# Splitting the weight blocks of a hybrid encoder kernel: one instruction per part of a whole block, in place of one per part of each half

## The chip, the cores and the metric

The kernel runs on one core of one Trainium2 chip. The metric is the device time of one execution in microseconds. The kernel before took 910.26 us, the median of three runs (910.05 to 911.16). The engines of the core are named as in the profile: PE is the matrix engine (PEld its loads of the stationary operand), DVE the vector engine, ACT the scalar engine, POOL the general engine, and SP the queue that issues most of the transfers.

## What is computed

One layer of an encoder on 512 tokens of width 1024, all in float32. A combined projection feeds three mixers (a bidirectional mLSTM, a two-dimensional neighbourhood attention, a cross-attention into 256 memory tokens). Their outputs are gated, summed and projected, and a gated feed-forward block of inner width 2816 follows. Cut to what matters:

```python
h = rms_norm(x, mix_norm_g)
proj = h @ w_in                       # 1024 x 7184
...                                   # the three mixers
merged = g_ml * (y_ml @ w_br_ml) + g_na * (y_na @ w_br_na) + g_xa * (y_xa @ w_br_xa)
x = x + merged @ w_out
a, u = split(rms_norm(x, ffn_norm_g) @ w_ffn_up)      # 1024 x 5632
x = x + (gelu(dwconv3(a, w_conv, b_conv)) * u) @ w_ffn_down   # 2816 x 1024
return rms_norm(x, final_norm_g)
```

## The kernel before

**Three matmuls for one.** Every dense product is done in a float32 kind that the matrix engine reads rounded. So each operand is split into a high part (the value, rounded by a copy into that kind) and a low part (what the rounding lost), and `mm3` (line 201) issues three matmuls for each k tile of 128 rows: high weights by high input (L202), high weights by low input (L203), low weights by high input (L204). The input's parts are made once and stay in buffers called units. The weights' parts are made block by block, just ahead of their use.

**Blocks.** `block_list` (line 53) cuts all weights into 159 blocks in the order of use. Nearly all are 128 partitions by 1024 columns: for a projection these are the 8 k tiles of one output tile, side by side. The 2816 rows of the down projection are 22 k tiles, done in two passes of 11 (`HF`); one output tile in one pass takes two blocks, of 8 and of 3 k tiles (1024 and 384 columns, line 82). Three blocks called `dnl` hold the weights of the last two output tiles of the second pass; their parts go into units that are kept to the end (`lastw`, line 160).

**A block's way.** `emit_raw` (line 141) loads a block into one of 3 raw buffers by a transfer that SP issues. `emit_split` (line 167) makes the parts, half a block at a time: for a half of 512 columns one ACT copy writes the high part (L184), and one DVE subtraction writes the low part (L185). Each half has a buffer of its own; there are 4 for the high and 4 for the low parts, of 544 columns each (`HWD`). `weights(key)` (line 190) is called just before a block's matmuls. It emits loads up to three blocks ahead and splits up to one block ahead.

**Order.** The program is written in one order, but a scheduler reorders each engine's instructions by when it expects them to be ready, earlier written ones first, and gives a buffer to the next user when it expects it to be free. An engine then runs its list strictly in that order. A split of a half can start when some buffer has been released by the last matmul that read it: L203 for a high part, L204 for a low part.

**The stages**, by the trace: the q and k projections and the values (to about 98 us), the projections of the mixers with the mLSTM's steps between them (to 310), the gates with the neighbourhood attention between them (to 420), the last gates and the output projection (to 531), and the feed-forward block. There `ua` and `uu` are the two halves of the up projection, one block each per tile `f`, and `dn` is the down projection: 11 tiles of `ua` and `uu` to 655, 8 tiles of `dn` to 716, 11 tiles of `ua` and `uu` to 838, and 5 of `dn` to 876. From there the last three output tiles are done in halves of 256 columns and rows, with the final norm between (`last_tiles`, line 980).

Two places differ from the regular course. At tile `f` = 0 of the up projection (lines 1088 to 1104) both blocks are in use at once: 7 k tiles of `ua`, 7 of `uu`, then the last of `ua`, eight small matmuls for the norm (L283), and the last of `uu`. And in the stage of the values, `mem_part` (line 393) loads and splits the memory tokens in four steps (L396, L398, L208, L209) on the same engines as the weights.

Of the kernel before, what the change touches and what calls it, by code (L numbers as in the profile page):

```python
# [11 lines left out]
F32 = mybir.dt.float32  # L12
F32R = mybir.dt.float32r
AF = mybir.ActivationFunctionType
ALU = mybir.AluOpType
AX = mybir.AxisListType

P = 128
# [7 lines left out]
HF = FT // 2  # L26
# [5 lines left out]
EPS = 1e-6  # L32
NEG = -1e30
BW = 1088
HWD = 544
UNIT = 2064
ROWS, GW = 8, 64
CW = (0, 8, 24, 32)
# [14 lines left out]
def block_list():  # L53

    L = []
    for i in range(4):
        L.append((("mlq", i), 1024))
    for f in range(4):
        L.append((("mlk", f), 1024))
    for c in range(4):  # L60
        n = 272 if c == 0 else 256
        for h in range(2):
            L.append((("tm", c, h), 4 * n))
    for n in ("xaq", "o", "memk", "memv", "naq", "nak"):
        for f in range(4):
            L.append(((n, f), 1024))
    for br in range(3):
        for fp in range(4):
            L.append((("g", br, 2 * fp), 1024))
            L.append((("g", br, 2 * fp + 1), 1024))  # L70
            L.append((("br", br, fp), 1024))
    for f in range(8):
        L.append((("out", f), 1024))
    for hh in range(2):
        for f in range(HF * hh, HF * (hh + 1)):
            L.append((("ua", f), 1024))
            L.append((("uu", f), 1024))
        for f in range(8 if hh == 0 else LF):
            if hh == 1 and f >= LF - 3:
                i = f - LF + 3  # L80
                L.append((("dnl", i), 256 * (4 if i < 2 else 3)))
            for i, n in ((0, 8), (1, 3)):
                L.append((("dn", hh, f, i), n * 128))
    return L


BLOCKS = block_list()
BINDEX = {}
_off = 0
# [4 lines left out]
BCOLS = {n: (lambda k: P) for n in ("mlk", "o", "xaq", "memk", "naq", "nak", "g", "out", "ua", "uu", "dn")}  # L94
# [7 lines left out]
def hybrid_block(ctx, tc, xT, memT, wflat, vecs, gbias, nabias, outa, outb):  # L102
    nc = tc.nc
    V, A, G, PE, SY = nc.vector, nc.scalar, nc.gpsimd, nc.tensor, nc.sync

    cp = ctx.enter_context(tc.tile_pool(name="cp", bufs=1))
    wp = ctx.enter_context(tc.tile_pool(name="wp", bufs=3))
# [9 lines left out]
    def nm(s):  # L117
        uid[0] += 1
        return f"{s}_{uid[0]}"

    def unit(dt=F32):
        return up.tile([P, UNIT], dt, tag="unit", name=nm("u"))
# [14 lines left out]
    raws, split = {}, {}  # L137
# [11 lines left out]
            return [(r[:, a:b], src[:, a:b]) for a, b in zip(cuts, cuts[1:])]  # L149
        SY.dma_start(r[:, :n], src)  # L150

    def halves(i):
        n, c = BLOCKS[i][1], BCOLS[BLOCKS[i][0][0]](BLOCKS[i][0])
        k = n // c
        k0 = k if n <= HWD else (k + 1) // 2
        return c, [(0, k0)] + ([(k0, k)] if k0 < k else [])

    lw = []

    def lastw(k, m):  # L160

        if not lw:
            lw.extend(unit(F32R) for _ in range(4))
        q = slice(k % 8 * 256, k % 8 * 256 + m)
        return lw[k // 8][:, q], lw[2 + k // 8][:, q]

    def emit_split(i):
        key, n = BLOCKS[i]
        r = raws.pop(i)
        c, hs = halves(i)  # L170
        split[i] = []
        for a, b in hs:
            m = (b - a) * c
            if key[0] == "dnl":
                h, l = lastw(4 * key[1] + a, m)
            else:
                h = wp.tile([P, HWD], F32R, tag="hi", name=nm("wh"), bufs=4)
                l = wp.tile([P, HWD], F32R, tag="lo", name=nm("wl"), bufs=4)
            for u, v in ((0, P), (P, m)) if i == 0 and a == 0 else ((0, m),):
                src = r[:, a * c + u:a * c + v]  # L180
                if i == 0 and a == u == 0:
                    V.tensor_copy(h[:, u:v], src)
                else:
                    A.activation(h[:, u:v], src, AF.Copy)  # L184
                V.tensor_tensor(l[:, u:v], src, h[:, u:v].bitcast(F32), op=ALU.subtract)  # L185
            for k in range(a, b):
                q = slice((k - a) * c, (k - a + 1) * c)
                split[i].append((h[:, q], l[:, q]))

    def weights(key):  # L190

# [67 lines left out]
    for d in range(2):  # L259
        sgn = 1 if d == 0 else -1  # L260
        m = cp.tile([P, P], F32, name=f"msk{d}")
# [81 lines left out]
    for k in range(KT):  # L343
# [5 lines left out]
        wh, wl = ws[k % 2]  # L349
# [64 lines left out]
    for c in range(4):  # L414
        if c == 3:
            mem_part()
        n = 272 if c == 0 else 256
# [467 lines left out]
    for f in range(4):  # L885
        ps = proj(("naq", f), XH, XL)
        V.tensor_tensor(nq[:, f * S:(f + 1) * S].rearrange("p (b r c) -> p b r c", r=ROWS, b=4), rv(ps), rv(rb),
                        op=ALU.mult)
# [15 lines left out]
    for br in range(3):  # L904
# [8 lines left out]
        for fp in range(4):  # L913
            tg = []
            for i in range(2):
                f = 2 * fp + i
# [11 lines left out]
            for i in range(2):  # L928
                f = 2 * fp + i
# [152 lines left out]
    for hh in range(2):  # L1082
# [3 lines left out]
        for j in range(HF):  # L1086
            f = HF * hh + j
            if f == 0:
# [7 lines left out]
                k = KT - 1  # L1096
# [8 lines left out]
            c = conv(pa, rb2, "ffw", "ffb", f, FT)  # L1105
# [33 lines left out]
def _layout(inp):  # L1139
    w_in = inp["w_in"][0]  # L1140
    o_ml = 0
    c_q, c_k, c_v, c_o = 0, 512, 1024, 1536
    c_g = 2048
    c_nq, c_nk, c_nv = 2064, 2064 + 512, 2064 + 1024
    c_xq = 2064 + 1536
    c_m = c_xq + 512
    wi = _tiles(w_in)
    mkv = _tiles(inp["w_mem_kv"][0])
    br = [_tiles(inp[n][0]) for n in ("w_br_ml", "w_br_xa", "w_br_na")]
    wo = _tiles(inp["w_out"][0])  # L1150
    wu = _tiles(inp["w_ffn_up"][0])
    wd = _tiles(inp["w_ffn_down"][0])
    parts = []
    for key, n in BLOCKS:
        kind = key[0]
        if kind == "mlq":
            b = wi[:, 2 * key[1]:2 * key[1] + 2, c_q:c_q + 512]
        elif kind in ("mlk", "o", "xaq", "naq", "nak"):
            c = {"mlk": c_k, "o": c_o, "xaq": c_xq, "naq": c_nq, "nak": c_nk}[kind] + key[1] * P
            b = wi[:, :, c:c + P]  # L1160
        elif kind == "tm":
            _, c, h = key
            ks = slice(4 * h, 4 * h + 4)
            if c == 0:
                b = np.concatenate([wi[:, ks, c_g:c_g + 16], wi[:, ks, c_v:c_v + 256]], axis=2)
            elif c == 1:
                b = wi[:, ks, c_v + 256:c_v + 512]
            else:
                b = wi[:, ks, c_nv + (c - 2) * 256:c_nv + (c - 1) * 256]
        elif kind == "memk":  # L1170
            b = mkv[:, :, key[1] * P:(key[1] + 1) * P]
        elif kind == "memv":
            b = mkv[:, 2 * key[1]:2 * key[1] + 2, 512:1024]
        elif kind == "g":
            gi = (0, 2, 1)[key[1]]
            c = c_m + gi * 1024 + key[2] * P
            b = wi[:, :, c:c + P]
        elif kind == "br":
            b = br[key[1]][:, :, key[2] * 256:(key[2] + 1) * 256]
        elif kind == "out":  # L1180
            b = wo[:, :, key[1] * P:(key[1] + 1) * P]
        elif kind == "ua":
            b = wu[:, :, key[1] * P:(key[1] + 1) * P]
        elif kind == "uu":
            b = wu[:, :, DFF + key[1] * P:DFF + (key[1] + 1) * P]
        elif kind == "dnl":
            k = HF + 4 * key[1]
            b = wd[:, k:k + n // 256, LF * P:]
        else:
            _, hh, f, i = key  # L1190
            b = wd[:, HF * hh + 8 * i:HF * hh + 8 * i + n // P, f * P:(f + 1) * P]
        parts.append(np.ascontiguousarray(b).reshape(-1))
    wflat = np.concatenate(parts)

    vt = lambda a: a.reshape(-1, P).T
    vecs = np.concatenate([vt(inp["mix_norm_g"][0]), vt(inp["ffn_norm_g"][0]), vt(inp["mem_norm_g"][0]),
                           vt(inp["final_norm_g"]),
                           vt(inp["w_ml_conv"][0].reshape(-1)), vt(inp["b_ml_conv"][0]), vt(inp["b_merge_gate"][0]),
                           vt(inp["w_ffn_conv"][0].reshape(-1)), vt(inp["b_ffn_conv"][0]), vt(inp["ml_norm_g"][0])], axis=1)
    bi, bf = inp["b_ml_igate"][0], inp["b_ml_fgate"][0]  # L1200
    gbias = np.concatenate([bi[0], bf[0], bi[1], bf[1], inp["final_norm_g"][LF * P:]])

    rpb = inp["na_rpb"][0]
    q = np.arange(P)
    qr, qc = q // 16, q % 16
    kk = np.arange(M)
    kr, kc = kk // 32, kk % 32
    nab = np.empty((8, P, 4, M), rpb.dtype)
    for b in range(4):
        c = 16 * b + qc  # L1210
        cols = CW[b] + kc
        start = np.clip(c - 8, 0, GW - 16)
        ok = (cols[None, :] >= start[:, None]) & (cols[None, :] < start[:, None] + 16)
        dr = kr[None, :] - qr[:, None] + 7
        dc = np.clip(cols[None, :] - c[:, None] + 15, 0, 30)
        nab[:, :, b, :] = np.where(ok[None], rpb[:, dr, dc], rpb.dtype.type(NEG))

    xT = _tiles(np.ascontiguousarray(inp["x"][0].T))
    memT = _tiles(np.ascontiguousarray(inp["mem"][0].T))
    return {"xT": xT, "memT": memT, "wflat": wflat, "vecs": vecs, "gbias": gbias, "nabias": nab.reshape(8, P, 2, 2 * M).transpose(0, 2, 1, 3)}  # L1220
# [17 lines left out]
```

## Time and profile before

| | |
|---|---|
| runs | 910.05, 910.26, 911.16 us |
| the profiled execution's own time | 909.93 us |
| its span in the profile | 908.1 us |
| granted PE clock, mean over the span | 0.998 |
| PE busy | 900.4 us, 4502 matmuls |
| PEld busy | 755.2 us |
| DVE busy | 579.5 us, 1059 instructions |
| ACT busy | 436.8 us, 884 instructions |
| POOL busy | 107.5 us |
| read from memory | 92.57 MB, 105 GB/s with what is written |

The 1.8 us between span and time lie around the first and last recorded instruction. Matmuls overlap, so their durations (0.39 us for 512 columns) are longer than the distance between the starts of two, and it is the distance that fills the span. In rows of the timeline the columns are start in us, duration in us, engine, line, operation, output and inputs, shape, count, and in brackets the engine's idle time before it with what ended that.

### The profile page before, as it was taken

The numbers are of one execution on the slowest core, as the hardware profiler recorded it, in microseconds if no ns is written. First come the engines' busy times: TensorE is split into PE (matmuls) and PEld (weight loads), VectorE is DVE, ScalarE is ACT, GpSimd is POOL, SyncE is SP. The second block draws the span as 40 slices with busy tenths as digits, with TensorE's granted clock in tenths as the row PEclk, the third lists the DMA queues.
The fourth block names the chain that finished last, engine by engine and source line by source line (L and its number), as shares of the span: only waits on it lengthen the run. The fifth ranks groups of instructions, "written<-read, shape, count | busy, mean of one in ns | idle before, by whom it ended". The sixth has DMA issues, their size and how long they took to land.

```text
span 908.1 us, 12239 instructions
## 1 busy us (share of the span) xinstructions
PE 900.4 (99%) x4502; PEld 755.2 (83%) x4502; DVE 579.5 (64%) x1059; ACT 436.8 (48%) x884; POOL 107.5 (12%) x136
## 2 busy tenths in 40 slices
PE   9999999999999999999999999999999999999997
PEld 7899888888888888888888888888888888888887
DVE  6794656746566758885555548777733477777433
ACT  7474546755545647654334435444422244444442
POOL 4200311102040300000000221111100011111010
PEclk9999999999999999999999999999999999999999
DMA  7223543422232333232223432222233322322312
GB/s 264 96 71 119 182 119 116 156 89 82 91 119 71 114 105 127 95 117 70 93 93 117 139 116 93 93 93 92 88 96 96 116 93 93 93 93 87 119 49 93
DMA packets 33339, 96.52 MB, mean 106 GB/s; under 512 B 4344, under 2 KB 7672, under 8 KB 33280
## 3 DMA queue, kind: packets, MB, share of 16 engines
q1 hardware_dynamic: 31584, 92.32, 31.5%
q0 software_dynamic: 1408, 3.16, 1.2%
q8 instruction: 35, 0.57, 0.3%
q10 hardware_dynamic: 288, 0.27, 0.1%
q14 instruction: 24, 0.20, 0.1%
HBM read 92.57 MB, written 3.16 MB: 105 GB/s over the span
## 4 chain that ended last, share of the span: by engine, by line
PE 96%; DVE 1%; issue 1%; ACT 1%; DMA 1%; SPq 0%; POOLq 0%; POOL 0%; DVEq 0%
PE mm L202 28%; PE mm L203 28%; PE mm L204 28%; PE at L202 2%; PE at L203 2%; PE at L204 2%; PE at L580 2%; PE at L718 1%; PE at L705 1%; DMA s<-xT 1%; PE at L795 0%; PE at L688 0%; PE at L687 0%; PE at L283 0%; PE at L604 0%
## 5 line engine op out<-in xcount | busy, mean ns | idle before, releaser
L202 PE MATMUL mm<-u,wh 128*128 128x512 f32 (+1 forms) x1077 | 420.6, 391 | 0.5 <-ACT u L208 0.3
L203 PE MATMUL mm<-u,wh 128*128 128x512 f32 (+1 forms) x1077 | 417.4, 388 | 0.3 <-DVE u L209 0.3
L204 PE MATMUL mm<-u,wl 128*128 128x512 f32 (+1 forms) x1077 | 417.2, 387 | 0.0
L184 ACT ACTIVATE wh<-wr 128x512 fp32r<-128x512 f32 (+1 forms) x298 | 185.6, 624 | 285.6 <-PE mm L203 241.5
L185 DVE TENSOR_TENSOR wl<-wr,wh 128x512 fp32r<-128x512 f32 (+3 forms) x299 | 228.7, 766 | 121.4 <-ACT wh L184 114.9
L204 PEld LDWEIGHTS mm<-u,wl 128*128 128x128 f32 x1077 | 202.2, 188 | 45.2 <-DVE wl L185 0.4
L202 PEld LDWEIGHTS mm<-u,wh 128*128 128x128 f32 x1077 | 202.3, 188 | 44.2 <-ACT u L208 0.6
L203 PEld LDWEIGHTS mm<-u,wh 128*128 128x128 f32 x1077 | 202.4, 188 | 43.9 <-DVE u L209 1.3
L1111 POOL TENSOR_TENSOR s<-s,rb 128x512 f32<-128x512 f32 x22 | 29.1, 1323 | 266.4 <-DVE s L1110 258.3
L208 ACT ACTIVATE u<-s 128x512 fp32r<-128x512 f32 x34 | 21.4, 630 | 53.1 <-DVE s L1114 50.6
L964 POOL TENSOR_TENSOR acc<-acc,s 128x512 f32<-128x512 f32 x7 | 9.1, 1298 | 223.1 <-ACT s L963 223.1
L209 DVE SCALAR_TENSOR_TENSOR u<-s,u 128x512 fp32r<-128x512 f32 x34 | 23.5, 692 | 14.9 <-ACT u L208 14.6
L919 DVE TENSOR_TENSOR s<-mm,rb_x 128x512 f32<-128x512 f32 x24 | 16.6, 690 | 23.6 <-PE mm L204 23.5
L568 ACT ACTIVATE E<-R,bi 128x128 f32<-128x128 f32 x80 | 27.8, 393 | 4.2 <-POOL R L549 4.0
L369 ACT ACTIVATE s<-pad,vec 128x512 f32<-128x512 f32 x30 | 24.4, 812 | 8.3 <-DVE pad L367 8.3
L370 DVE SCALAR_TENSOR_TENSOR s<-pad,vec,s 128x512 f32<-128x512 f32 x30 | 22.5, 751 | 6.1 <-ACT s L369 6.0
L202 PE MATMUL mm<-wh,u 128*128 128x256 f32 (+1 forms) x80 | 24.5, 306 | 0.0
L203 PE MATMUL mm<-wl,u 128*128 128x256 f32 (+1 forms) x80 | 24.3, 304 | 0.0
L204 PE MATMUL mm<-wh,u 128*128 128x256 f32 (+1 forms) x80 | 24.3, 304 | 0.0
L1110 DVE SCALAR_TENSOR_TENSOR s<-s,s 128x512 f32<-128x512 f32 x22 | 15.2, 692 | 13.4 <-ACT s L1109 13.3
L371 DVE SCALAR_TENSOR_TENSOR s<-pad,vec,s 128x512 f32<-128x512 f32 x30 | 22.5, 750 | 0.7
L367 DVE TENSOR_TENSOR pad<-mm,rb 128x512 f32<-128x512 f32 x22 | 15.1, 692 | 11.6 <-PE mm L204 11.6
(261 smaller groups left out, 1003.2 us busy)
## 6 DMA issues: line engine op xcount, KB each, us to landing
wr<-wflat SPq DMA_DIRECT2D x140, 512.0 KB, 3.4
s<-xT SPq DMA_DIRECT2D x16, 256.0 KB, 4.3
nab<-nabias SPq DMA_DIRECT2D x16, 256.0 KB, 2.7
wr<-wflat SPq DMA_DIRECT2D x15, 192.0 KB, 2.4
R<-rd SPq DMA_DIRECT2D x8, 256.0 KB, 3.5
u<-nav_d POOLq DMA_DIRECT2D x32, 64.0 KB, 2.9
wr<-wflat SPq DMA_DIRECT2D x2, 544.0 KB, 3.3
s<-memT SPq DMA_DIRECT2D x4, 256.0 KB, 3.6
```

The costliest lines, as they stand in the source:

```text
L184: A.activation(h[:, u:v], src, AF.Copy)
L185: V.tensor_tensor(l[:, u:v], src, h[:, u:v].bitcast(F32), op=ALU.subtract)
L202: PE.matmul(ps, lh, rh, start=start, stop=False)
L203: PE.matmul(ps, lh, rl, start=False, stop=False)
L204: PE.matmul(ps, ll, rh, start=False, stop=stop)
L208: A.activation(h, src, AF.Copy, scale=scale)
L209: V.scalar_tensor_tensor(l, src, scale, h.bitcast(F32), op0=ALU.mult, op1=ALU.subtract)
L369: A.activation(t1, pad[:, 0:512], AF.Identity, scale=vcol(w, i), bias=vcol(b, i))
L370: V.scalar_tensor_tensor(t1, pad[:, 1:513], vcol(w, n + i), t1, op0=ALU.mult, op1=ALU.add)
L371: V.scalar_tensor_tensor(t1, pad[:, 2:514], vcol(w, 2 * n + i), t1, op0=ALU.mult, op1=ALU.add)
L568: A.activation(E[:, i, :], src, AF.Exp, bias=bi[:, d, abs(J - s), s, h:h + 1])
L1111: G.tensor_tensor(c, c, rb2, op=ALU.mult)
```

## The change

A whole block is split by one ACT copy and one DVE subtraction, into one of 2 high and 2 low buffers of 1088 columns each. Only the first two blocks are still cut, at the borders at which their transfers are cut. The blocks of the down projection hold 6 and 5 k tiles (768 and 640 columns) in place of 8 and 3. The loads, their buffers, the matmuls and everything else in the program stay as they were; the columns of the `dnl` blocks go to the same places.

```diff
-HWD = 544
+KA = 6
...
-            for i, n in ((0, 8), (1, 3)):
+            for i, n in ((0, KA), (1, HF - KA)):
                 L.append((("dn", hh, f, i), n * 128))
...
-    def halves(i):
-        n, c = BLOCKS[i][1], BCOLS[BLOCKS[i][0][0]](BLOCKS[i][0])
-        k = n // c
-        k0 = k if n <= HWD else (k + 1) // 2
-        return c, [(0, k0)] + ([(k0, k)] if k0 < k else [])
...
     def emit_split(i):
         key, n = BLOCKS[i]
         r = raws.pop(i)
-        c, hs = halves(i)
-        split[i] = []
-        for a, b in hs:
-            m = (b - a) * c
-            if key[0] == "dnl":
-                h, l = lastw(4 * key[1] + a, m)
+        c = BCOLS[key[0]](key)
+        if key[0] == "dnl":
+            h, l = lastw(4 * key[1], n)
+        else:
+            h = wp.tile([P, BW], F32R, tag="hi", name=nm("wh"), bufs=2)
+            l = wp.tile([P, BW], F32R, tag="lo", name=nm("wl"), bufs=2)
+
+        cuts = ((0, P, n // 2, n), (0, n // 2, n))[i] if i < 2 else (0, n)
+        for u, v in zip(cuts, cuts[1:]):
+            if i == u == 0:
+                V.tensor_copy(h[:, u:v], r[:, u:v])
             else:
-                h = wp.tile([P, HWD], F32R, tag="hi", name=nm("wh"), bufs=4)
-                l = wp.tile([P, HWD], F32R, tag="lo", name=nm("wl"), bufs=4)
-            for u, v in ((0, P), (P, m)) if i == 0 and a == 0 else ((0, m),):
-                src = r[:, a * c + u:a * c + v]
-                if i == 0 and a == u == 0:
-                    V.tensor_copy(h[:, u:v], src)
-                else:
-                    A.activation(h[:, u:v], src, AF.Copy)
-                V.tensor_tensor(l[:, u:v], src, h[:, u:v].bitcast(F32), op=ALU.subtract)
-            for k in range(a, b):
-                q = slice((k - a) * c, (k - a + 1) * c)
-                split[i].append((h[:, q], l[:, q]))
+                A.activation(h[:, u:v], r[:, u:v], AF.Copy)
+            V.tensor_tensor(l[:, u:v], r[:, u:v], h[:, u:v].bitcast(F32), op=ALU.subtract)
+        split[i] = [(h[:, k:k + c], l[:, k:k + c]) for k in range(0, n, c)]
...
-            b = wd[:, HF * hh + 8 * i:HF * hh + 8 * i + n // P, f * P:(f + 1) * P]
+            b = wd[:, HF * hh + KA * i:HF * hh + KA * i + n // P, f * P:(f + 1) * P]
```

## The prediction

> **What bounds the kernel now.** I read the page first, then the waits, then the groups by shape, then the timeline at the places where the change could bite.
>
> ```profile
> span 908.1 us, 12239 instructions
> PE 900.4 (99%) x4502; PEld 755.2 (83%) x4502; DVE 579.5 (64%) x1059; ACT 436.8 (48%) x884; POOL 107.5 (12%) x136
> PE 96%; DVE 1%; issue 1%; ACT 1%; DMA 1%; SPq 0%; POOLq 0%; POOL 0%; DVEq 0%
> L204 PEld LDWEIGHTS mm<-u,wl 128*128 128x128 f32 x1077 | 202.2, 188 | 45.2 <-DVE wl L185 0.4
> ACT wh L184 <- PE mm L203: 241.5, 176, 3.8
> DVE wl L185 <- ACT wh L184: 114.9, 105, 4.2
> ```
>
> The matrix engine is busy from end to end, and 96% of the chain that ended last is matmuls. The weight parts are not what it waits for: loads of low parts lost 0.4 us to the split in the whole run. It is the other way round: ACT stood 241.5 us waiting until matmuls released a high buffer. So a cheaper split buys nothing by itself. The time can move only through two things: stalls of PE that a later split would bring, and the distance between matmuls that follow each other without a stall.
>
> **What a split costs, narrow and wide.**
>
> ```profile
> L184 ACT ACTIVATE wh<-wr 128x512 fp32r<-128x512 f32 x279 | 175.1, 629 | 262.8 <-PE mm L203 223.2 <-DMA wr<-wflat 10.2 <-issue 9.5
> L184 ACT ACTIVATE u<-wr 128x256 fp32r<-128x256 f32 x1 | 0.4, 401 | 0.0
> L185 DVE TENSOR_TENSOR u<-wr,u 128x512 fp32r<-128x512 f32 x5 | 3.4, 690 | 5.6 <-ACT u L184 5.6
> L185 DVE TENSOR_TENSOR u<-wr,u 128x256 fp32r<-128x256 f32 x1 | 0.4, 424 | 0.0
> L1121 DVE TENSOR_TENSOR u<-mm,u 128x512 f32<-128x512 f32 x13 | 9.0, 692 | 14.8 <-PE mm L204 14.8
> wr<-wflat SPq DMA_DIRECT2D x140, 512.0 KB, 3.4
> ```
>
> No row has 1024 columns. From 256 to 512 columns ACT adds 0.228 us and DVE 0.266 us, so the wide ones take 0.629 + 2 x 0.228 = 1.08 us and 0.690 + 2 x 0.266 = 1.22 us. The bounds are no fixed part at all, twice the narrow one (1.26 and 1.38 us), and, below, the narrow one itself. For 768 and 640 columns the same line gives 0.86 and 0.74 us on ACT, 0.96 and 0.82 on DVE. Some 0.17 us of ACT and 0.16 us of DVE are saved for each block; both lie beside matmuls and are worth nothing.
>
> **How late a block becomes.** A row of the steady course, block `uu` of a tile and the block after it:
>
> ```profile
> 588.10 0.63 ACT L184 ACTIVATE wh<-wr 128x512 fp32r<-128x512 f32 x1 [0.18 <-PE mm L203]
> 588.72 1.28 POOL L1111 TENSOR_TENSOR s<-s,rb 128x512 f32<-128x512 f32 x1 [8.69 <-DVE s L1110]
> 588.76 1.78 DVE L185 TENSOR_TENSOR wl<-wr,wh 128x512 fp32r<-128x512 f32 x1
> 593.57 0.40 PE L202 MATMUL mm<-u,wh 128*128 128x512 f32 x1
> 599.18 0.39 PE L202 MATMUL mm<-u,wh 128*128 128x512 f32 x1
> 604.67 0.40 PE L202 MATMUL mm<-u,wh 128*128 128x512 f32 x1
> 610.28 0.39 PE L202 MATMUL mm<-u,wh 128*128 128x512 f32 x1
> ```
>
> 593.57 starts the `uu` block, 599.18 the `ua` block, 604.67 `uu` again. The second half of the 593.57 block got its buffer at 588.10, where the block two before ended. Its first half had got its own half a block earlier. In the new kernel all of it begins at 588.10: high part ready at 589.2, low part at 590.4, or 591.5 with the 1.09 us (1.78 less 0.69) that the subtraction loses beside POOL. It is needed at 593.57, its low part at 594.0. Before, the second half was ready at 588.73 (high) and 590.54 (low) for a use half a block after 593.57, at 596.4: a slack of 7.6 and 5.8 us. It falls to 4.4 and 2.5, and no stall follows. What is queued behind the longer wait are the evacuations and the activation chain on ACT and DVE; they get 0.5 us more delay, and the matmuls that need their results (the down projection) come many blocks later. The raw buffer comes free about 1 us later, so SP's next load starts that much later; it takes 3.4 us and has two blocks of time.
>
> [...]
>
> In the down projection a block has 6 k tiles or 5. Twenty-four matmuls take 5.5 us, so 6 k tiles take 4.2 and 5 take 3.5. The 6-tile block's buffer is released 3.5 us before its use: 3.5 - 0.86 - 0.96 leaves 1.7 us. The 5-tile block has 4.2 us, less 0.74, 0.82 and one evacuation of 0.69 on DVE: 1.9 us. No stall, with 8 and 3 or with 6 and 5.
>
> **Two places with less room.** First, tile 0 of the up projection, where two blocks are held together.
>
> ```profile
> 541.59 0.63 ACT L184 ACTIVATE wh<-wr 128x512 fp32r<-128x512 f32 x1 [2.11 <-PE mm L203]
> 542.69 0.69 DVE L185 TENSOR_TENSOR wl<-wr,wh 128x512 fp32r<-128x512 f32 x1
> 543.23 0.39 PE L202 MATMUL mm<-u,wh 128*128 128x512 f32 x1
> 543.68 0.39 PE L204 MATMUL mm<-u,wl 128*128 128x512 f32 x1
> ```
>
> At 541.59 the last k tile of `ua` gave its buffer back. The block needed at 543.23 had been split before; with two buffers it can only start then. High part 541.59 + 1.08 = 542.67, low part to 543.95 with a small instruction between, wanted at 543.68. A stall of **0.35 us** (0 with the narrow duration, 0.7 with the doubled ones).
>
> Second, the step from the values to the mixers:
>
> ```profile
> 97.52 0.63 ACT L184 ACTIVATE wh<-wr 128x512 fp32r<-128x512 f32 x1
> 101.57 0.63 ACT L398 ACTIVATE s<-s 128x512 f32<-128x512 f32 x1 [2.88 <-DMA s<-memT]
> 102.91 1.66 ACT L184 ACTIVATE wh<-wr 128x512 fp32r<-128x512 f32 x3
> 103.59 0.39 PE L202 MATMUL mm<-u,wh 128*128 128x512 f32 x1
> 104.05 0.39 PE L204 MATMUL mm<-u,wl 128*128 128x512 f32 x1
> 104.11 1.28 DVE L185 TENSOR_TENSOR wl<-wr,wh 128x512 fp32r<-128x512 f32 x2
> ```
>
> The first half of the block used at 103.59 was copied at 97.52; its second half stood in ACT's list behind the last step of the memory tokens, whose load came late, to 102.91. The whole block now goes to one of these two places. Ahead: no stall. Behind: high part 102.91 + 1.08 = 103.99, low part 104.11 + 1.22 = 105.33, wanted at 104.05: 1.3 us, or 1.9 if the later raw release pushes the memory load behind it by 0.6. I take **0**: ACT is idle when the buffer comes free (97.52 to 101.57 holds one short evacuation besides), and a scheduler that takes what is ready would fill that. The other value is a rival.
>
> **The distance between matmuls.** The rows from 599.18 to 604.67 and on to 610.28 hold the same work: 24 matmuls of 512 columns, the same inputs, no stall. `ua` takes 5.49 us and `uu` 5.61, tile after tile. What differs is where the weights lie. Tile 0 shows it: the release at 541.59 is of the second buffer of `ua`, taken out of turn. Counting the buffers as they come free, `ua` since then sits in buffers 0 and 2 and `uu` in 1 and 3. Buffers are 544 columns apart, so in units of 32 columns they start at 0, 17, 34 and 51: `ua` in the even places, `uu` in the odd. In the new kernel the halves of the two buffers start at 0, 16, 34 and 50, all even. If the place is the cause, all 22 `uu` blocks take `ua`'s time: 21 x 0.12 = **-2.5 us** (tile 0 left out). The other end is that all go at `uu`'s pace: +2.6 us.
>
> More rows show the down projection, a projection of the mixers, and the first of the last tiles:
>
> ```profile
> 860.80 0.39 PE L202 MATMUL mm<-u,wh 128*128 128x512 f32 x1
> 868.43 0.39 PE L202 MATMUL mm<-u,wh 128*128 128x512 f32 x1
> 123.32 0.39 PE L202 MATMUL mm<-u,wh 128*128 128x512 f32 x1
> 126.11 0.39 PE L202 MATMUL mm<-u,wh 128*128 128x512 f32 x1
> 128.87 0.40 PE L202 MATMUL at<-u,u 128*128 128x512 f32 x1
> 876.03 0.28 PE L202 MATMUL mm<-u,wh 128*128 128x256 f32 x1
> 878.39 0.28 PE L204 MATMUL mm<-u,wl 128*128 128x256 f32 x1
> ```
>
> Eleven k tiles of `dn` take 7.63 us; at `ua`'s pace they would take 5.49 x 11 / 8 = 7.55. Over 13 tiles that is at most -1.0 us; I take **-0.3**, as the buffers rotate and only half the blocks lie in odd places. In the mixers' stage the first half of the block (even) takes 2.79 us and the second (odd) 2.76, the other way round than in the feed-forward block, so the place of the input counts too. Should the second halves slow down to 2.79, 44 such blocks lose 44 x 0.03 = 1.3 us; should they stay, nothing. I take **+0.6**.
>
> **The sum**, on the profiled execution's own 909.93 us: +0.35 - 2.5 - 0.3 + 0.6 = -1.85, which gives 908.1 us. The median of the runs is 0.33 us above that execution, so **908.4 us** against 910.26. The start (the first two blocks keep their cuts) and the tail are unchanged: the last 5-tile block gets its buffer at 876.03 and has both parts after 0.74 + 0.82 and an evacuation of 0.69, at 878.3; its low part is first wanted at the seventh k tile, 878.39.
>
> **The rivals.**
>
> *The place of the weights does nothing* (the 0.12 us comes from something else that stays, such as the output bank or the place of the inputs, and `uu` keeps 5.61). For it: the mixers' rows point the other way. Against it: `ua` and `uu` have the same inputs. Then only the stall is left: 910.26 + 0.35 = 910.6 us. [...] Rows of 5.49 / 24 = 229 and 5.61 / 24 = 234 ns do not agree with a single distance.
>
> *The stall at the memory tokens comes, and the spacing does not*: 910.26 + 0.35 + 1.3 to 1.9 = 911.9 to 912.5, **912.2 us**, slower. For it: the second half was put behind that step before. It decides as soon as ACT's list has the copy behind L398. With the spacing gained as well it would be 910.0.
>
> *All blocks fall into the slow class*: +2.6 in the up projection, +1.3 in the mixers' stage, +0.35: 914.5 us. For it: the even place is the slow one in the mixers' rows. Against it: the even place is the fast one in the 22 tiles.
>
> **The chances.** A measurement of this kernel tells no less than 0.2% from no change, 1.8 us. Forecast 0.45; it lies on that bound, so I count 0.33 of it as faster and 0.12 as within. Spacing unmoved: 0.27, within. Stall with or without the gain: 0.16, of it 0.11 slower, 0.03 within, 0.02 faster (the mixers' stage improving too). Slow class: 0.12, slower. Waits not foreseen, from lists put in another order, take 0.04 from "within" to slower. Together: faster 0.35, within 0.38, slower 0.27. The range goes from 906.2 (-2.5, -1.0 and -0.6 in the mixers' stage, without the stall) to 913.5, short of the slow class. The forecast's own range is 906.5 to 909.8.
>
> **What would show it.** `uu` at 5.49 us like `ua` shows the spacing right; both at 5.61, or unchanged, shows it wrong. The first copy after tile 0's first blocks should be 1.08 us long, and the wait of PE for L185 at that place 0.35 us. The copy ahead of L398 shows the second place right, behind it wrong. Splits of 1.08 and 1.22 us show the durations. A PE idle for several us between stages, for splits or for transposes of the mixers, would make the whole prediction wrong.

## The result, and the profile after

| | before | after |
|---|---|---|
| median of the runs | 910.71 us (6 runs, 909.97 to 911.33) | 915.18 us (6 runs, 912.50 to 915.71) |
| profiled execution, its span | 909.93, 908.1 us | 915.34, 913.6 us |
| instructions of DVE, ACT | 1059, 884 | 916, 741 |

The medians are 4.5 us apart. The ratio of the two kernels, by all their runs, is 1.0044, 95% interval 1.0034 to 1.0054: the change makes the kernel about 0.44% slower, where 908.4 us had been predicted and 913.5 was the end of the range. In the changed kernel `mm3` is at L192 to L194, the split at L176 on ACT and L177 on DVE. The busy line of its page:

```profile
PE 902.9 (99%) x4502; PEld 758.3 (83%) x4502; DVE 562.4 (62%) x916; ACT 410.0 (45%) x741; POOL 114.5 (13%) x136
```

The waits of PE (total in us, times, longest):

```profile
PE mm L194 <- DVE wl L177: 1.8, 1, 1.8
PE mm L193 <- DVE u L199: 0.9, 1, 0.9
PE mm L192 <- ACT wh L176: 0.5, 1, 0.5
```

ACT and DVE do get cheaper (ACT busy 436.8 to 410.0 us), and a wide copy takes 1.06 us against 1.08 estimated. But PE has three waits that it did not have, or, for the second, had at 0.3 us. The largest is one wait of 1.8 us for a low part, between tiles 2 and 3 of the up projection. PE, ACT and DVE there, from the timeline (start, duration, engine, line, and in brackets the idle time before):

```profile
564.55 1.04 ACT L176 ACTIVATE wh<-wr 128x1024 fp32r<-128x1024 f32 x1
...
567.92 0.69 DVE L1104 TENSOR_TENSOR s<-mm,s 128x512 f32<-128x512 f32 x1 [0.86 <-POOL s L1101]
568.53 0.68 DVE L199 SCALAR_TENSOR_TENSOR u<-s,u 128x512 fp32r<-128x512 f32 x1
...
570.13 0.39 PE L193 MATMUL mm<-u,wh 128*128 128x512 f32 x1
571.06 1.22 DVE L177 TENSOR_TENSOR wl<-wr,wh 128x1024 fp32r<-128x1024 f32 x1
572.33 0.51 PE L194 MATMUL mm<-u,wl 128*128 128x512 f32 x1 [1.81 <-DVE wl L177]
```

The high part was ready at 565.6. Its subtraction stands in DVE's list behind the activation steps of earlier tiles, some of which themselves wait for POOL, and so starts at 571.06, 5.5 us later. PE wanted it at 570.36, one matmul distance (0.23 us) after the last start, and gets it at 572.33.

What comes after that wait is as large. Three stretches of 3.4 us (length, busy time and count of PE, PEld, DVE, ACT and POOL, the granted clock of PE, the share and rate of the DMA):

```profile
569.50:572.90 3.40, 1.59 (x7) 1.00 (x6) 3.40 (x6) 1.58 (x2) 0.00 (x0) 1.00 0.00 0
572.90:576.30 3.40, 3.40 (x10) 2.65 (x9) 1.96 (x3) 0.63 (x1) 1.28 (x1) 0.51 0.77 218
576.30:579.70 3.40, 3.40 (x16) 2.81 (x15) 1.57 (x3) 1.24 (x2) 0.00 (x0) 0.99 0.22 90
```

In the second stretch PE is busy throughout and does 10 matmuls where the third does 16: the granted clock is one half. That costs 1.6 us, so this place takes 3.6.

The two other waits are at the start and at tile 0:

```profile
19.41 1.23 DVE L177 TENSOR_TENSOR wl<-wr,wh 128x1024 fp32r<-128x1024 f32 x1 [3.81 <-ACT wh L176]
20.55 3.48 DVE L199 SCALAR_TENSOR_TENSOR u<-s,vec,u 128x512 fp32r<-128x512 f32 x2
22.38 0.50 PE L193 MATMUL mm<-u,wh 128*128 128x512 f32 x1 [0.86 <-DVE u L199]
545.13 1.06 ACT L176 ACTIVATE wh<-wr 128x1024 fp32r<-128x1024 f32 x1 [8.11 <-issue]
546.22 1.23 DVE L177 TENSOR_TENSOR wl<-wr,wh 128x1024 fp32r<-128x1024 f32 x1
546.66 1.06 ACT L176 ACTIVATE wh<-wr 128x1024 fp32r<-128x1024 f32 x1 [0.48 <-PE mm L193]
546.93 0.40 PE L193 MATMUL mm<-u,wh 128*128 128x512 f32 x1
547.76 1.22 DVE L177 TENSOR_TENSOR wl<-wr,wh 128x1024 fp32r<-128x1024 f32 x1 [0.32 <-ACT wh L176]
547.78 0.50 PE L192 MATMUL mm<-u,wh 128*128 128x512 f32 x1 [0.45 <-ACT wh L176]
548.35 0.39 PE L194 MATMUL mm<-u,wl 128*128 128x512 f32 x1
```

At the start the low part of x, which PE needs, stands behind a wide subtraction that has time. At tile 0 a wait was foreseen, but for another part. The copy at 545.13 and the subtraction at 546.22 are those of the block needed next, `ua` of tile 1. Its low part was ready at 547.45, and after the matmul at 546.93 it would have been wanted at 547.16: 0.3 us, as foreseen. But in PE's list the first two matmuls of `uu` of tile 1 now come before that use. Their copy could only begin at 546.66, when `uu` of tile 0 was done, and PE waits for it until 547.78. The L194 at 548.35 is that of `ua`: the low part of `uu`, begun at 547.76, was not ready before 548.98.

The distances between matmuls, where the prediction saw a gain: the second half of a block of the mixers, and a `uu` block of the up projection up to the block after it, in the changed kernel.

```profile
128.97 0.40 PE L192 MATMUL mm<-u,wh 128*128 128x512 f32 x1
131.77 0.40 PE L192 MATMUL at<-u,u 128*128 128x512 f32 x1
601.05 0.39 PE L192 MATMUL mm<-u,wh 128*128 128x512 f32 x1
606.54 0.39 PE L192 MATMUL mm<-u,wh 128*128 128x512 f32 x1
```

`uu`, from 601.05 to 606.54, now takes 5.49 us like `ua`; that gain came. The mixers' second half went from 2.76 to 2.80.

Where the time went, by setting each matmul of one trace against the same matmul of the other. The two profiled executions are 5.41 us apart, more than the medians, and the last matmul that reads weights starts 5.45 us later:

| stretch | after, less before |
|---|---|
| first 24 matmuls | +1.3 us |
| low part of x, at 21 us | +0.9 |
| mixers' stage, distance of the matmuls | +1.7 |
| tile 0 of the up projection | +0.6 |
| wait between tiles 2 and 3 | +2.0 |
| half clock after it | +1.6 |
| feed-forward part, distance of the matmuls | -2.3 |

The rows sum to 5.8; the rest, -0.35 us, is small differences elsewhere. The first row is no effect of the change. Busy time and count of PE from 2 to 13 us, before and after:

```profile
2.00:13.00 11.00, 10.25 (x42) 7.74 (x42) 6.38 (x13) 7.48 (x13) 1.96 (x11) 1.00 0.94 314
```
```profile
2.00:13.00 11.00, 10.58 (x36) 8.33 (x36) 6.60 (x13) 7.59 (x13) 1.96 (x11) 1.00 0.91 307
```

Six matmuls fewer, because the first ones ran slower for longer: from 6.1 to 9.5 us their starts are 0.43 us apart, where before most are 0.23 apart from 5.8 us on. In the kernels below the count was 41 or 42 in four and 35 to 38 in the others, and it did not go with what was changed: the kernel with the third low buffer has the same lists as the changed one and did 41.

### The profile page after: what moved, and what is told of

It reads as the page before. It is cut to its first block, busy times and chain, and to the rows that moved or that the text cites. A ratio compares the mean times of both kernels' runs of the same rounds, so it can differ in the third digit from the quotient of the medians.

```text
span 913.6 us, 11777 instructions
## 1 busy us (share of the span) xinstructions
PE 902.9 (99%) x4502; PEld 758.3 (83%) x4502; DVE 562.4 (62%) x916; ACT 410.0 (45%) x741; POOL 114.5 (13%) x136
## 5 line engine op out<-in xcount | busy, mean ns | idle before, releaser
L192 PE MATMUL mm<-u,wh 128*128 128x512 f32 (+1 forms) x1077 | 422.5, 392 | 0.9 <-ACT wh L176 0.5
L194 PE MATMUL mm<-u,wl 128*128 128x512 f32 (+1 forms) x1077 | 418.1, 388 | 1.8 <-DVE wl L177 1.8
L176 ACT ACTIVATE wh<-wr 128x1024 fp32r<-128x1024 f32 (+4 forms) x158 | 157.9, 999 | 269.1 <-PE mm L193 164.9
L177 DVE TENSOR_TENSOR wl<-wr,wh 128x1024 fp32r<-128x1024 f32 (+5 forms) x159 | 201.6, 1268 | 102.2 <-ACT wh L176 102.0
L194 PEld LDWEIGHTS mm<-u,wl 128*128 128x128 f32 x1077 | 203.1, 189 | 47.3 <-DVE wl L177 2.2
L192 PEld LDWEIGHTS mm<-u,wh 128*128 128x128 f32 x1077 | 203.3, 189 | 43.5 <-ACT wh L176 0.9
L954 POOL TENSOR_TENSOR acc<-acc,s 128x512 f32<-128x512 f32 x7 | 12.6, 1801 | 218.0 <-ACT s L953 218.0
L1097 ACT ACTIVATE s<-s 128x512 f32<-128x512 f32 x22 | 13.9, 632 | 41.4 <-DVE s L361 41.3
L192 PE MATMUL mm<-wh,u 128*128 128x256 f32 (+1 forms) x80 | 24.6, 307 | 0.0
L194 PE MATMUL mm<-wh,u 128*128 128x256 f32 (+1 forms) x80 | 24.3, 304 | 0.0
L1098 DVE SCALAR_TENSOR_TENSOR s<-s,s 128x512 f32<-128x512 f32 x22 | 15.2, 691 | 14.0 <-ACT s L1097 14.0
L1100 DVE SCALAR_TENSOR_TENSOR s<-s,s 128x512 f32<-128x512 f32 x22 | 15.2, 691 | 13.3 <-ACT s L1099 13.3
L361 DVE SCALAR_TENSOR_TENSOR s<-pad,vec,s 128x512 f32<-128x512 f32 x30 | 22.5, 751 | 0.9
```

The costliest lines, as they stand in the source:

```text
L176: A.activation(h[:, u:v], r[:, u:v], AF.Copy)
L177: V.tensor_tensor(l[:, u:v], r[:, u:v], h[:, u:v].bitcast(F32), op=ALU.subtract)
L192: PE.matmul(ps, lh, rh, start=start, stop=False)
L194: PE.matmul(ps, ll, rh, start=False, stop=stop)
L361: V.scalar_tensor_tensor(t1, pad[:, 2:514], vcol(w, 2 * n + i), t1, op0=ALU.mult, op1=ALU.add)
```

## The experiments

The theories: the waits come from **where a wide subtraction stands in DVE's list**; the distances come from **the place of the buffers**. The rivals: two whole buffers leave too little time whatever the list; wide instructions disturb the matmuls; place does nothing. Each kernel was timed together with the kernel before on the same chip.

### The place alone

The kernel before, with narrow splits and four buffers, and only the distance of the buffers changed:

```diff
-                h = wp.tile([P, HWD], F32R, tag="hi", name=nm("wh"), bufs=4)
+                h = wp.tile([P, HWD + 32], F32R, tag="hi", name=nm("wh"), bufs=4)[:, OFF:OFF + HWD]
```

and `l` likewise, with `OFF` 0 (all even) or 32 (all odd).

> The kernel before with its narrow splits and four half buffers; only the distance of the buffers is changed, from 544 to 576 columns, so that all start at even multiples of 32 columns (0, 18, 36, 54). Theory (the place sets the distance of the matmuls): the uu blocks go from 5.61 to 5.50 us for 24 matmuls (22 blocks, -2.4 us), the second halves of the mixers' blocks from 230 to 233 ns for a matmul (+1.7 us), no new wait of PE; 909.0 to 910.0 us against 910.3. Rival (place does nothing, what came with the change came from the wide instructions): uu stays at 5.61 us, the second halves at 230 ns, and the time within 0.5 us of before.

> The same as the even kernel, but the weights lie 32 columns further into each buffer, so that all start at odd multiples of 32 columns. Theory: ua slows from 5.49 to 5.60 us like uu (+2.4 us), the first halves of the mixers' blocks go from 232.5 to 230 ns (-1.5 us or so); 911 to 912 us. Rival (place does nothing): no distance moves by more than 0.5 ns and the time stays at 910.3 us.

Measured: even 909.48 us against 911.04, ratio 0.9983 (0.9975 to 0.9992); odd 911.26 us, 1.0002 (0.9993 to 1.0011). A `uu` block and the starts around it, first even, then odd:

```profile
594.54 0.39 PE L203 MATMUL mm<-u,wh 128*128 128x512 f32 x1
600.04 0.39 PE L203 MATMUL mm<-u,wh 128*128 128x512 f32 x1
```
```profile
594.10 0.40 PE L203 MATMUL mm<-u,wh 128*128 128x512 f32 x1
599.70 0.40 PE L203 MATMUL mm<-u,wh 128*128 128x512 f32 x1
```

Even: 5.50 us for `uu`, and 5.49 for the `ua` block after it. Odd: 5.60 in this first pass over the tiles. In the mixers it is the other way round (the table below: 232 and 233 ns even, 230 odd). Neither has a wide instruction, and the even one gives the changed kernel's distances in both stages. Even and odd differ in nothing but the 32 columns by which the weights are moved. The place is the cause, and the mixers want the other place than the up projection.

The changed kernel, with the second half of the blocks ahead of the output projection moved to an odd place, still written by one instruction:

```diff
+        if 2 <= i < BINDEX[("out", 0)][0] and n == 1024:
+            hg, lg, rg = (t.rearrange("p (a b) -> p a b", a=2) for t in (h, l, r[:, :n]))
+            A.activation(hg[:, :, :512], rg, AF.Copy)
+            V.tensor_tensor(lg[:, :, :512], rg, hg[:, :, :512].bitcast(F32), op=ALU.subtract)
+            at = [k + 32 * (k >= 512) for k in range(0, n, c)]
...
```

> The changed kernel, its wide splits and two whole buffers; for the blocks of 1024 columns ahead of the output projection the second half lies 32 columns further on (at 544 instead of 512, an odd place), still written by one instruction with a gap. Theory: the mixers' second halves go from 233 back to 230 ns, 1.2 to 1.7 us less, all waits stay: 913.5 to 914.0 us against 915.2. Rival (the 1.7 us in the mixers' stage come from the wide instructions, which disturb the matmuls' reads): the second halves stay at 233 ns, 915.2 us.

Measured: 911.68 us, ratio 1.0007 (0.9998 to 1.0016). The second half of the mixers' block takes 2.76 us again, so the 1.7 us are the place's:

```profile
127.02 0.39 PE L199 MATMUL mm<-u,wh 128*128 128x512 f32 x1
129.78 0.40 PE L199 MATMUL at<-u,u 128*128 128x512 f32 x1
569.27 0.50 PE L201 MATMUL mm<-u,wl 128*128 128x512 f32 x1 [1.82 <-DVE wl L184]
```

It came out 2 us below what was expected, although the wait of 1.8 us is there. In the trace no half clock follows it:

```profile
565.10:568.50 3.40, 2.35 (x11) 1.59 (x9) 3.40 (x6) 1.02 (x2) 0.00 (x0) 1.00 0.00 0
568.50:571.90 3.40, 2.63 (x11) 2.17 (x12) 3.06 (x4) 1.83 (x3) 0.21 (x1) 1.00 0.45 153
```

Here the wait lies across the border of two stretches of the clock's record, 1.05 us of idle time in one and 0.77 in the other (3.40 less the busy time); in the changed kernel all of it lay in one. The half clock that is missing is worth 1.6 of the 2 us; the rest is within what the first matmuls differ by. That the border is the reason is an inference from these traces, which the last section takes up.

The best place for each stage, in the kernel before (narrow splits):

```diff
+                o = 32 if i < BINDEX[("out", 0)][0] and key[0] != "br" else 0
...
```

> The kernel before, narrow splits and four half buffers of 576 columns; only the place in the buffer changes by block: 32 columns in (odd place) for all blocks ahead of the merge's output projection except the br blocks, 0 (even place) for the br blocks and from the output projection on. Theory (each stage has its fast place; the two kernels before showed both): the feed-forward part as in the even kernel (uu at 5.50 us), the mixers' part as in the odd kernel (2.9 us less than in the even one), br at 231.6 ns: 906.3 us, between 905.5 and 907.5, against 910.3 to 911.0 for before. Rival (the gains of the two kernels don't add): not under 908.5 us.

Measured: 906.59 us against 910.89, ratio 0.9947 (0.9935 to 0.9959). The gains add.

Last, the even kernel with the buffers of the inputs elsewhere:

```diff
-UNIT = 2064
+UNIT = 2080
```

> The kernel with all weight buffers at even places, and the buffers that hold the matmuls' inputs 2080 instead of 2064 columns long, so that the inputs lie elsewhere and the weights where they were; the lists are the same. Theory (the distance hangs on the place of weights and inputs together, which is why the mixers and the feed-forward part want opposite places): the distance changes by more than 1 ns in at least one of ua/uu (228.9 ns) and the mixers' blocks (233 ns), and the time by more than 0.5 us. Rival (the weights' place alone counts): all distances within 0.5 ns, 909.5 us.

Measured: 904.18 us against 910.17, ratio 0.9930 (0.9918 to 0.9943), the fastest of all. The weights are where they were in the even kernel, and a `uu` block takes 5.44 us:

```profile
591.26 0.39 PE L203 MATMUL mm<-u,wh 128*128 128x512 f32 x1
596.70 0.39 PE L203 MATMUL mm<-u,wh 128*128 128x512 f32 x1
```

So the place of the inputs counts with that of the weights; longer input buffers also move whatever the program lays out behind them, which this run does not separate. The mean distance of undisturbed 512-column matmuls, in ns, from the traces (24 of them make a block):

| kernel | `g`, k tiles 0 to 3 | `g`, 4 to 7 | `ua` | `uu` | second pass of `dn` |
|---|---|---|---|---|---|
| before | 232.0 | 230.5 | 229.0 | 233.5 | 231.0 |
| changed | 232.1 | 232.8 | 229.0 | 229.0 | 229.9 |
| even, narrow | 231.8 | 232.9 | 228.9 | 228.9 | 229.9 |
| odd, narrow | 229.6 | 230.1 | 232.2 | 232.2 | 233.1 |
| even, inputs moved | 229.7 | 229.2 | 226.8 | 226.7 | 232.2 |

### The wait between tiles 2 and 3

The changed kernel, the subtraction put further up in DVE's list for the up projection only:

```diff
+            if key[0] in ("ua", "uu"):
+                with tc.high_priority():
+                    V.tensor_tensor(l[:, u:v], r[:, u:v], h[:, u:v].bitcast(F32), op=ALU.subtract)
```

> The changed kernel with one thing else: the subtraction of the low part of the ua and uu blocks is given priority in the scheduler's list. Theory (the 1.8 us wait between tiles 2 and 3 comes from the place of that subtraction in DVE's list, and the half clock follows from the wait): the wait of PE for L177 there goes, the 3.4 us of half clock go with it, 3.4 to 3.8 us less: 911.4 to 911.8 us against 915.2. Rival (two whole buffers leave too little time whatever the list): a wait of over 1 us stays somewhere in tiles 1 to 4, and the time stays above 914 us.

The changed kernel with a third low buffer, and the lists of all engines as they were:

```diff
-            l = wp.tile([P, BW], F32R, tag="lo", name=nm("wl"), bufs=2)
+            l = wp.tile([P, BW], F32R, tag="lo", name=nm("wl"), bufs=3)
```

> The changed kernel with three whole buffers for the low parts instead of two (paid for with five of the twelve buffers of 32 columns); the lists of all engines are the same as in the changed kernel. Theory (place in DVE's list): the third buffer doesn't help, the wait of 1.8 us between tiles 2 and 3 and the half clock stay, 915.2 us. Rival (too few buffers): the wait goes, and the time falls to 911.6 us.

Measured: with priority 911.75 us, ratio 1.0008 (0.9999 to 1.0016); with the third buffer 914.60 us, 1.0037 (1.0024 to 1.0050). The subtraction on DVE with priority, then the stretch of the wait and the one after it with the third buffer:

```profile
566.87 1.99 DVE L179 TENSOR_TENSOR wl<-wr,wh 128x1024 fp32r<-128x1024 f32 x1
```
```profile
568.60:572.00 3.40, 1.60 (x8) 1.00 (x7) 3.40 (x6) 1.67 (x3) 0.00 (x0) 1.00 0.00 0
572.00:575.40 3.40, 3.40 (x10) 2.63 (x9) 1.96 (x3) 0.55 (x1) 1.27 (x1) 0.50 0.79 252
```

Priority moves the subtraction from 571.06 to 566.87 (drawn out to 1.99 us, beside a multiplication of POOL from 566.49 to 567.78); PE has no wait there and no half clock, and 3.7 us are gone at that place. A third low buffer changes nothing there: PE waits 1.8 us for L177 as before. The list is the cause, not the low buffers' number. The high buffers were two in both runs, so a third one for both parts, which would let the copy itself start earlier, stays untried.

Two whole buffers, with two narrow instructions for each part:

```diff
-        cuts = ((0, P, n // 2, n), (0, n // 2, n))[i] if i < 2 else (0, n)
+        m = n if n <= 544 else (n // c + 1) // 2 * c
+        cuts = (0, P, m, n) if i == 0 else (0, m, n) if m < n else (0, n)
```

> The changed kernel's two buffers of a whole block and blocks of six and five k tiles, but two narrow instructions for each part as before. Theory (the length of the instruction and its place in DVE's list make the wait between tiles 2 and 3; the first half's subtraction stands further up in this list and takes 0.69 us): that wait falls under 0.7 us, no half clock; the wait at tile 0 falls from 0.62 to 0.2 us or less; 910.5 to 912.5 us. Rival (the two whole buffers alone make the waits): over 1 us of wait stays between tiles 2 and 3, and 0.5 at tile 0; 914 to 915.2 us.

Measured: 911.79 us, ratio 1.0007 (0.9998 to 1.0016). The waits at tile 0 and between tiles 2 and 3 are gone, as expected. But two others came, by the waits of PE:

```profile
PE mm L194 <- DVE u L200: 1.4, 1, 1.4
PE mm L195 <- DVE wl L178: 0.5, 1, 0.5
```

The second of them in the timeline, at the step of the memory tokens (`L389` is its last load's copy):

```profile
105.16 0.63 ACT L389 ACTIVATE s<-s 128x512 f32<-128x512 f32 x1 [3.36 <-DMA s<-memT]
106.50 2.18 ACT L177 ACTIVATE wh<-wr 128x512 fp32r<-128x512 f32 x4
107.16 0.50 PE L193 MATMUL mm<-u,wh 128*128 128x512 f32 x1 [0.30 <-ACT wh L177]
```

The wait for the low part of x at the start is longer (1.4 us), and here the copies do stand behind the step of the memory tokens, the place that the prediction's second rival named: 1.2 us over the usual distances. So it is the wide instruction at its place in the list that makes the waits in the up projection: narrow ones remove both waits there, and priority for the wide one removes the larger. Whole buffers alone already give the scheduler other lists, with waits elsewhere.

The wide kernel with all remedies (the first of the versions below), without the priority for `ua` and `uu`:

```diff
-            if key[0] in ("ua", "uu"):
-                with tc.high_priority():
-                    V.tensor_tensor(l[:, u:v], r[:, u:v], h[:, u:v].bitcast(F32), op=ALU.subtract)
-            else:
-                V.tensor_tensor(l[:, u:v], r[:, u:v], h[:, u:v].bitcast(F32), op=ALU.subtract)
+            V.tensor_tensor(l[:, u:v], r[:, u:v], h[:, u:v].bitcast(F32), op=ALU.subtract)
```

> The last wide kernel without the priority for the subtractions of the ua and uu blocks; priority for x and the places stay. Theory: the wait of 2.0 us between tiles 2 and 3 comes back, 908.4 us, and 1.6 us more (910.0) in those executions where 3.4 us of half clock follow it, which happens where the whole wait lies in one stretch of the clock's record. Rival (in this kernel the lists have other room, the priority did nothing): 906.5 us, no wait.

Measured: 909.77 us, ratio 0.9989 (0.9980 to 0.9998), against 906.44 with it. PE waits 1.8 us for L178; the two stretches that hold the wait:

```profile
563.60:567.00 3.40, 2.91 (x13) 2.06 (x11) 3.09 (x5) 0.94 (x2) 0.27 (x1) 1.00 0.00 0
567.00:570.40 3.40, 2.09 (x9) 1.74 (x10) 3.40 (x5) 2.21 (x3) 0.00 (x0) 1.00 0.33 100
```

The wait is back, and in the trace no half clock follows it: PE is idle for 0.5 and 1.3 us in two stretches. The rival is out; the priority is worth the wait. That the time comes near the theory's second value, 910.0, is luck: in the trace the first matmuls lose 1.8 us against the kernel with priority, and the half clock nothing. How often the half clock follows can't be read from the times of this kernel, as they mix it with what the first matmuls lose.

### The blocks of the down projection

The changed kernel, wide splits and two buffers:

```diff
-KA = 6
+KA = 8
```

> The changed kernel with the down projection's blocks back at eight and three k tiles. Theory (the six and five k tiles do nothing): 914.9 us, within 0.4% of the changed kernel's, no wait of PE in the down projection in either. Rival (six and five were needed once a block is split whole): waits of PE for a split in the down projection, over 916.5 us. The wait of 2 us between tiles 2 and 3 stays by both.

Measured: 918.15 us, ratio 1.0085 (1.0072 to 1.0099). The time is the rival's: 3 us slower than the changed kernel. PE waits for a low part at three places, at two of which the changed kernel doesn't. The first of these, then ACT at the same place in the changed kernel:

```profile
856.65 1.06 ACT L176 ACTIVATE u<-wr 128x1024 fp32r<-128x1024 f32 x1 [3.47 <-DMA wr<-wflat]
857.62 1.46 ACT L176 ACTIVATE wh<-wr 128x1024 fp32r<-128x1024 f32 x2
858.89 1.22 DVE L177 TENSOR_TENSOR wl<-wr,wh 128x1024 fp32r<-128x1024 f32 x1
860.16 0.50 PE L194 MATMUL mm<-u,wl 128*128 128x512 f32 x1 [0.72 <-DVE wl L177]
```
```profile
855.09 0.85 ACT L176 ACTIVATE wh<-wr 128x768 fp32r<-128x768 f32 x1 [1.78 <-PE mm L193]
856.03 1.06 ACT L176 ACTIVATE u<-wr 128x1024 fp32r<-128x1024 f32 x1
```

With eight and three, the split of an eight-tile block stands in the lists behind the split of a resident block for the last tiles (`dnl`, the rows with `u`), and that one waits 3.47 us for its load. In the changed kernel the resident block's split comes second at both places, and PE does not wait. So this too is an order of the lists together with a late load; whether blocks of eight and three k tiles would wait in another order is not shown. Matmul by matmul, the trace falls 2.2 us behind the changed kernel's at these two places.

### Versions that beat both

The changed kernel with priority for `ua` and `uu`, the same for the split of x, and the best place for each stage:

```diff
+            o = 32 if i < BINDEX[("out", 0)][0] and key[0] != "br" else 0
+            h = wp.tile([P, BW + 64], F32R, tag="hi", name=nm("wh"), bufs=2)[:, o:o + BW]
...
+        with tc.high_priority():
+            split_act(XH[k], XL[k], xk[k], vcol("mix_g", k))
```

> The changed kernel with all that the other runs point to: priority for the subtraction of the ua and uu blocks, priority for the split of x at the start (its low part then stands ahead of the wide subtraction that delayed it by 0.9 us), and odd places for the blocks ahead of the output projection except br. Theory: 911.75 of the kernel with priority, less 0.9 at the start, less 2.9 in the mixers: 908.0 us, between 907.2 and 908.8; the wait at tile 0 (0.62 us) stays. Rival (wide instructions cost something apart from lists and places): not under 909.5 us.

Measured: 906.44 us, ratio 0.9954 (0.9941 to 0.9966). The wait at 21 us is gone, the one at tile 0 stays. The same with all weights at even places, as in the changed kernel, and `UNIT = 2080`:

> The changed kernel (wide splits, two whole buffers at even places, six and five k tiles) with priority for the subtractions of ua and uu and for the split of x, and the buffers of the inputs 2080 columns long. Theory: wide and narrow differ only by waits; with the places alike the time is that of the narrow kernel with 2080 columns, 904.2 us, plus the wait at tile 0 of 0.6 us: 904.8, between 904.0 and 905.8, and ua and uu at 226.8 ns. Rival (a wide split costs more than its waits): not under 906.5 us.

Measured: 905.25 us against 910.58, ratio 0.9941 (0.9928 to 0.9955), 0.6 us behind the narrow kernel at the last matmul that reads weights, which is the size of the wait at tile 0 (0.5 us recorded, the only one for weights that is left). The medians are 1.1 us apart; about 0.4 us of that lies outside the recorded spans (2.2 us of the profiled execution here, 1.8 in the narrow kernel) and is not explained. Within the span, with the same places, wide and narrow differ by little more than that wait.

## Why the prediction was wrong

**"A cheaper split buys nothing by itself"**: right. ACT gave up 26.8 us of busy time and PE's end moved with its waits and distances alone.

**What a wide split costs** (1.08 and 1.22 us estimated): right, 1.057 us on ACT and 1.22 on DVE undisturbed.

**"It falls to 4.4 and 2.5, and no stall follows"**: this is the step that failed. The slack was taken in the steady course, from a row where DVE starts a subtraction as soon as its high part is ready. In tiles 2 and 3, where the activation steps of the first tiles are still being worked off after the norm's row, a subtraction waits 5.5 us in DVE's list, and a slack of 2.5 us does not cover that. In the kernel before, the two halves of this block (`ua` of tile 3) stood at two places of that list, counted off in the order of the blocks. The one needed first, at 566.34, was the earlier by 3.4 us:

```profile
560.17 0.69 DVE L185 TENSOR_TENSOR wl<-wr,wh 128x512 fp32r<-128x512 f32 x1
563.53 0.68 DVE L185 TENSOR_TENSOR wl<-wr,wh 128x512 fp32r<-128x512 f32 x1
```

The prediction counted what is queued behind the longer instruction, and not what the instruction is queued behind. It gave waits from lists put in another order a chance of 0.04.

**The half clock** was not in the prediction at all: the wait of 2.0 us cost 3.6 us in the changed kernel, where all of it lay in one stretch. In the clock's record of that kernel the half clock lasts 3413 ns, and PE was idle for 53% of the stretch before it (3.40 us less 1.59 busy).

**"A stall of 0.35 us" at tile 0**: 0.6 us, and another wait than the foreseen one. By the prediction's own rows the stall is 543.95 less 543.68, 0.27 us and not 0.35, and the low part of `ua` does come 0.3 us after the time at which it would have been wanted. But the scheduler put two matmuls of `uu` ahead of that use, and PE waits for their high part instead, whose buffer comes free later. That the lists of PE would change too was left out.

**"The start and the tail are unchanged"**: wrong by 0.9 us. The first two blocks keep their cuts, but the third and fourth are wide, and the low part of x stands behind one of them. The other 1.3 us at the start are chance.

**The step at the memory tokens**, taken as 0: right for the changed kernel; with narrow instructions in the same buffers the wait appears. Which of the two happens is the scheduler's.

**The distance of the matmuls**: -2.3 us measured for the feed-forward part against -2.8 taken; +1.7 for the mixers against +0.6. The mechanism was right and is shown by the even and odd kernels; the mixers' term was mis-sized, by counting 44 blocks of one kind and taking half of what they could lose.

**"No stall, with 8 and 3 or with 6 and 5"**: right for six and five, wrong for eight and three. The resident blocks, whose splits go through the same two engines and can stand ahead in their lists, were left out of that sum.

## What to carry to other kernels

Making instructions fewer and longer on engines that are not the bound saved nothing here (26.8 us of ACT's busy time went, and the kernel took 4.5 us more); it made each result late as a whole, and where the list of an engine is written ahead of time, it must be looked at where a backlog is worked off, not in the steady course. A wait on the matrix engine can cost nearly twice its length: 2.0 us cost 3.6 here where half clock followed. And where that engine is busy all the time, moving buffers by a few columns is worth trying: two sizes (576 and 2080 columns) gave 0.7% here.

## What was not expected of the hardware

- The distance between matmuls of 512 columns went from 226.7 to 233.5 ns by the place of the weight and input buffers alone, with the same instructions around them. Which places of the two are slow together stays open: the runs show that weights and inputs count together, no more.
- A wait of 1.97 us on PE was followed by 3.41 us of half clock in the traces of three kernels, where all of it lay in one stretch of the clock's record (53% of it idle in the changed kernel and in the one with the third low buffer), and not in two others, where it lay across two (31% and 23% idle in one, 14% and 39% in the other). The same wait thus cost 2.0 or 3.6 us. A stretch is read off the changed kernel's trace: the clock changes there at 9.74, 572.93, 576.35 and 910.85 us, and these lie 165, 1 and 98 times 3.413 us apart. In the traces of the kernel before and of the changed one, once the clock was full, half clock followed the stretches with PE idle for 53, 83 and 85%, the last two at the end of the program, and none of the others, all of which had 25% or less. It did not follow 49% at the end of the kernel with narrow splits in whole buffers, nor 54% (1.56 of 3.40 us busy) at the end of the kernel with the best place for each stage. How much idle time it takes is not shown. In the changed kernel five of six executions have a mean granted clock of 0.996 or 0.997; the sixth, at 912.50 us, has 0.999. Why all 11 executions of the kernel with the odd second halves were at 0.998 or 0.999 is open: if the border were all, the wait should have fallen into one stretch in some of them.
- The rate of the first matmuls differs by execution: full clock is reached between 4.0 and 10.7 us after the span's start in the traces (4.2 in the kernel before, 9.7 in the changed one), which moves the 24th matmul by up to 1.9 us and does not go with what was changed.
